# A hybrid trunk step on one core: the gated recurrence in pieces, the running sum of branches in DRAM, y split block by block

## The chip, the cores and the metric

One NeuronCore of a Trainium2 chip runs the whole kernel. The metric is the device time of one launch in microseconds. TensorE does matmuls, VectorE and GpSimd elementwise work, ScalarE activations; SyncE's queue (SP) issues every DMA.

## The reference, cut to what matters

Two layers over 1152 tokens (128 context tokens and 1024 latent ones), width 1024, everything in float32. In each layer one projection of the normed input h feeds three branches: A, windowed attention; B, a gated linear recurrence in both directions over 512 channels; C, differential attention. What a layer ends with is

```python
m = sigmoid(h @ w_merge)                   # three times 1024 columns
y = ( m[0] * ((oa * silu(g_a)) @ w_br_a)
    + m[1] * ((ob * silu(g_b)) @ w_br_b)
    + m[2] * ((oc * silu(g_c)) @ w_br_c))
x = x + gate * (y @ w_out)

# branch B, for each direction d
r, i = sigmoid(u @ wa + ba), sigmoid(u @ wx + bx)     # u: width-4 convolution of x_b
a = exp(-8 * r * softplus(-lam))
h_t = a_t * h_(t-1) + sqrt(1 - a_t**2) * (i * u)_t    # a scan along the tokens
```

The gate, and the shift and scale of the next layer's norm, come from a product of the conditioning vector with `mod_w`.

## The kernel before, in words

Every float32 operand of a matmul is split into a high and a low part (`split`, line 141: ScalarE copies the high part, GpSimd or VectorE subtracts), and `mm3` (L162) makes three matmuls of each product (L163, L164, L165). Tokens come in three chunks of 384, output columns in blocks of 128.

A layer has three stages. In `unit_phase` the attention branches are computed, and their gated outputs go to DRAM (`osp`), as do the inputs of the recurrence (`xsp`, `gsp`). In the **tail** there are 24 steps, eight column blocks j for each branch, in the order C, A, B. A step loads and splits its weights, and for each token chunk c runs a *merge* (24 matmuls against h, then a Tanh on ScalarE into `mg`, L971) and, one chunk behind (two from step 7 on), a *branch* (12 matmuls of the branch's output `oh`, `ol` with `wb`), whose result VectorE multiplies with `mg` and adds to the running sum `yr[j]` (L980 to L983, recorded at the helpers' lines L112 and L103). Eight `yr` tiles stay on chip until the end. Steps 22 and 23 (`tail_last`, L1018) do their six merges first, then for each chunk split all eight blocks of y. In **w_out** (L1060) y is multiplied with `w_out` in four column quarters, x is updated, and in the last quarter the next layer's h is made from it.

The recurrence (`lru`, L853) is done once for each of four column tiles `ct`: load x, weights, convolution into `u`, split of `u` (`luhl`), 48 matmuls into PSUM tag "t", Tanh, Exp, Tanh, Square, Sqrt, the scans (recorded at L860), the output to `osp[1]`. It is issued whole before steps 0, 2, 4 and 5 (`LRUN`), above the tail in priority, with its VectorE work at low priority (`late`, `LVO`).

`mod_chunk` (L295) makes three columns blocks of modulation: four or three loads of `mod_w`, 16 VectorE operations into `macc`, six small matmuls (L314). Layer 0 has eleven of them to do: four at steps 10, 13, 16 and 19 (`MODN`), seven in w_out (`MODW`).

A planner orders the instructions of each engine's queue: it plays the program through with its own idea of durations, and takes the ready instruction of the highest priority, which is its place in the program, moved forward by `tc.high_priority(offset)` (or back, with a negative one). Each engine then runs its queue strictly in that order. Tiles come from pools with a tag (`al`, sizes in `RINGS`, line 54): "S" has 26 tiles of 1152 columns, "P" 7, "W" 7 for weights, "D" 3, "Q" 2, "E" 2, "T" 2, "cx" and "tab" 1. An instruction whose tile finds none free is not placed until one is released. h holds 16 of the "S", a branch's output 8 tiles (`OTAG`, line 946).

Of the kernel before, what the change touches and what calls it, by code (L numbers as in the profile page):

```python
# [19 lines left out]
NTOK = 1152  # L20
# [10 lines left out]
LPO = 2500  # L31

LVO = -1600
# [31 lines left out]
def hybrid_dit_kernel(ctx, tc, I, O):  # L65
# [54 lines left out]
    xsp, gsp = (drp.tile([4, 128, NTOK], F32, name=n) for n in ("xsp", "gsp"))  # L120

# [731 lines left out]
    def lru(L, ct):  # L853
# [3 lines left out]

        def late(f, *args, **kw):
            with tc.high_priority(offset=LVO):
                f(*args, **kw)  # L860
        PIECES = ((0, 128), (128, 640), (640, NTOK))
        x = al("T", "lx", NTOK)

# [13 lines left out]
        A.activation(out=u, in_=x, func=AF.Identity, scale=cw(2), bias=cols[:, R_CB + ct:R_CB + ct + 1])  # L877
        for a0, a1 in PIECES:
            e0, e1 = (0, 128) if a0 == 0 else (128, NTOK)
            for j in (0, 1, 3):  # L880
                t0, t1 = max(a0, e0 + 2 - j), min(a1, e1 + 2 - j)
                late(stt, u[:, t0:t1], x[:, t0 + j - 2:t1 + j - 2], cw(j), u[:, t0:t1], ALU.mult, ALU.add)
        ra = [al("P", "lr", NTOK) for _ in range(2)]
        ri = [al("P", "li", NTOK), al("S", "li", NTOK)]
        for c in range(3):
            s = slice(384 * c, 384 * c + 384)
            uhl = al("D", "luhl", 2, 384)
            split(uhl[:, 0, :], uhl[:, 1, :], u[:, s])
            for d in range(2):
                for k, (dst, hb) in enumerate(((ra, D.hba), (ri, D.hbx))):  # L890
                    p = ps("t", 384)
                    m = 2 * k + d
                    mm3(p, wh[:, m, :], wl[:, m, :], uhl[:, 0, :], uhl[:, 1, :], True, True)
                    A.activation(out=dst[d][:, s], in_=p, func=AF.Tanh, scale=0.5,
                                 bias=hb[:, 4 * d + ct:4 * d + ct + 1])
                late(stt, ri[d][:, s], ri[d][:, s], 1.0, u[:, s], ALU.add, ALU.mult)
# [7 lines left out]
        for d in range(2):  # L904
            for c in range(2):
                s = slice(576 * c, 576 * c + 576)
                t = al("D", "lt2", 576)
                A.activation(out=t, in_=av[d][:, s], func=AF.Square)
                late(stt, ra[d][:, s], t, 1.0, ra[d][:, s], ALU.add, ALU.mult)
        for d in range(2):  # L910
            A.activation(out=ra[d], in_=ra[d], func=AF.Sqrt, scale=0.25)
        for d in range(2):
            a = av[d]
            st = cols[:, R_ST + 4 * d + ct:R_ST + 4 * d + ct + 1]
            for a0, a1 in PIECES if d == 0 else PIECES[:1] + PIECES[:0:-1]:
# [8 lines left out]
                if d:  # L924
                    s = slice(a1 - 1, a0 - 1 if a0 else None, -1)
                late(V.tensor_tensor_scan, out=ra[d][:, s], data0=a[:, s], data1=ri[d][:, s], initial=ini,
                     op0=ALU.mult, op1=ALU.add)
            e = 127 if d == 0 else 0
            late(V.tensor_copy, fin[:, 4 * d + ct:4 * d + ct + 1], ra[d][:, e:e + 1])
        res = ra[0]  # L930
        for c in range(3):
# [4 lines left out]
            late(stt, res[:, s], res[:, s], 0.5, g, ALU.mult, ALU.mult)  # L936
        dma(osp[1][ct], res)

# [7 lines left out]
    OTAG = {2: "SSSSSSSS", 0: "PPTTSSSS", 1: "SSSSSSSS"}  # L946

    def load_o(L, br):

        out = []  # L950
        for k in range(4):
            hi, lo = al(OTAG[br][2 * k], "oh", NTOK), al(OTAG[br][2 * k + 1], "ol", NTOK)
            out.append((hi, lo))
# [3 lines left out]
        return out  # L957
# [9 lines left out]
    YTAG = ["P", "P", "P", "P", "S", "Q", "Q", "tab"]  # L967
# [5 lines left out]
    def tail_branch(L, order, j, c, ohl, wb, m):  # L973
        p2 = ps("s", 384)
# [19 lines left out]
    def tail_step(L, br, order, j, o, lag):  # L994
# [3 lines left out]
        if order == 0:  # L998
            L.yr.append(al(YTAG[j], "yr", NTOK))
        for c in range(3):  # L1000
# [3 lines left out]
            def branch(c=c, m=m):  # L1004
                tail_branch(L, order, j, c, o[br], wb, m)
            L.late.append(branch)
            if len(L.late) > lag:
                L.late.pop(0)()

    def y_split(L, j, c):  # L1010
        if c == 0:
            th, tlo = {5: "SP", 6: "PP", 7: "QQ"}.get(j, "SS")
            L.y.append((al(th, "yh", NTOK), al(tlo, "yl", NTOK)))
# [4 lines left out]
    def tail_last(L, br, ohl):  # L1018

        ms = [al("T", "mg2", 3, 384) for _ in range(2)]  # L1020
        wbs = {}
        for j in (6, 7):
            mw = ws_load(w_in_cols(L.l, CMG + 1024 * br + 128 * j), KT)
            for c in range(3):
                tail_merge(L, br, j, c, mw, ms[j - 6][:, c, :])
# [246 lines left out]
```

## Time and profile before

| | us |
|---|---|
| median of 3 runs | 2887.47 (2887.15 to 2888.11) |
| the profiled execution | 2884.63 |
| its span | 2882.8 |
| TensorE busy in it | 2740.5 |
| VectorE busy | 1773.3 |
| ScalarE busy | 1284.2 |
| GpSimd busy | 924.8 |

The span goes from the first to the last instruction. PE is TensorE's matmuls, PEld its weight loads, DVE VectorE, ACT ScalarE, POOL GpSimd. Matmuls overlap in the pipeline, so a matmul's own duration is longer than the distance between two starts. The tail of layer 0 begins at about 807 us and its w_out at 1340, the tail of layer 1 at about 2240 and its w_out at 2770.

### The profile page before, as it was taken

How to read it: one execution, taken by the hardware profiler on the slowest of the kernel's cores; microseconds unless marked ns; L12 is line 12 of the kernel's file. 1: busy time of each engine (PE TensorE's matmuls, PEld its weight loads, DVE VectorE, ACT ScalarE, POOL GpSimd, SP SyncE). 2: the span in 40 equal slices, each digit the busy share in tenths (PEclk: the TensorE clock that was granted, in tenths of full speed). 3: DMA queues.
4: the chain of work that ended last, by engine and by line, in shares of the span. 5: the costliest groups of instructions: out<-in, count | busy, mean ns of one | idle time of the engine just before them, and what ended most of it. 6: DMA issues, size and time to landing. Idle time of an engine off the chain costs nothing.

```text
span 2882.8 us, 44242 instructions
## 1 busy us (share of the span) xinstructions
PE 2740.5 (95%) x16745; PEld 2648.5 (92%) x16745; DVE 1773.3 (62%) x4412; ACT 1284.2 (45%) x2577; POOL 924.8 (32%) x756
## 2 busy tenths in 40 slices
PE   8999999999998989998999999999999989999999
PEld 4889999999997989998989899998999989899989
DVE  5887878776646583116958887787665455311162
ACT  4464555566654631212144555555666456212110
POOL 1334354531234341213104252445212344322130
PEclk9999999999999999998999999999999999999999
DMA  6011011112222252114631010110112121311122
GB/s 228 25 33 34 19 32 42 36 48 74 70 73 65 65 159 68 52 39 144 195 100 36 22 34 19 33 48 31 55 64 80 63 70 60 114 44 49 49 90 85
DMA packets 231698, 190.74 MB, mean 66 GB/s; under 512 B 21746, under 2 KB 217660, under 8 KB 231484
## 3 DMA queue, kind: packets, MB, share of 16 engines
q1 hardware_dynamic: 231484, 187.92, 20.7%
q8 instruction: 131, 2.15, 0.3%
q14 instruction: 83, 0.68, 0.1%
HBM read 153.52 MB, written 34.35 MB: 65 GB/s over the span
## 4 chain that ended last, share of the span: by engine, by line
PE 71%; DVE 15%; ACT 5%; issue 4%; DMA 3%; POOL 1%; SPq 1%; DVEq 0%; ACTq 0%; POOLq 0%
PE ps_s L163 18%; PE ps_s L164 18%; PE ps_s L165 18%; PE ps_o L711 2%; PE ps_t L702 2%; DVE P L542 2%; PE ps_s L540 2%; DVE macc L112 2%; PE ps_t L569 1%; PE ps_s L541 1%; DMA modw<-in_mod_w_dram 1%; DVE lr L860 1%; DVE lr L112 1%; PE ps_o L164 1%; PE ps_s L662 1%
## 5 line engine op out<-in xcount | busy, mean ns | idle before, releaser
L163 PE MATMUL ps_s<-h,wsh 128*128 128x384 f32 x1920 | 660.0, 344 | 8.6 <-ACT mg L971 5.9
L165 PE MATMUL ps_s<-h,wsl 128*128 128x384 f32 x1920 | 654.4, 341 | 0.9 <-POOL wsl L103 0.9
L164 PE MATMUL ps_s<-h,wsh 128*128 128x384 f32 x1920 | 654.9, 341 | 0.0
L163 PEld LDWEIGHTS ps_s<-h,wsh 128*128 128x128 f32 x1920 | 364.3, 190 | 13.5 <-ACT mg L971 7.1
L165 PEld LDWEIGHTS ps_s<-h,wsl 128*128 128x128 f32 x1920 | 363.1, 189 | 2.0 <-POOL wsl L103 1.6
L164 PEld LDWEIGHTS ps_s<-h,wsh 128*128 128x128 f32 x1920 | 364.1, 190 | 0.6
L103 POOL TENSOR_TENSOR wsl<-wsraw,wsh 128x1024 fp32r<-128x1024 f32 x80 | 198.7, 2483 | 395.3 <-ACT wsh L100 229.6
L163 PE MATMUL ps_s<-uwh,h 128*128 128x384 f32 x864 | 296.9, 346 | 5.8 <-ACT h L100 2.8
L164 PE MATMUL ps_s<-uwl,h 128*128 128x384 f32 x864 | 293.9, 341 | 0.1
L165 PE MATMUL ps_s<-uwh,h 128*128 128x384 f32 x864 | 292.1, 344 | 0.0
L112 DVE SCALAR_TENSOR_TENSOR ps_s<-mg,ps_s 128x384 f32<-128x384 f32 x96 | 52.6, 559 | 359.7 <-PE ps_s L165 359.6
L103 POOL TENSOR_TENSOR qkraw<-qkraw,tab 128x384 f32<-128x384 f32 (+2 forms) x92 | 132.7, 1453 | 335.2 <-DVE qkraw L103 212.5
L542 DVE TENSOR_SCALAR_CACHE_REDUCE P<-ps_s 128x384 f32<-128x384 f32 (+1 forms) x400 | 205.5, 539 | 39.9 <-PE ps_s L541 38.7
L163 PE MATMUL ps_s<-oh,wb 128*128 128x384 f32 x576 | 196.0, 351 | 35.3 <-DVE yr L112 10.5
L103 DVE TENSOR_TENSOR PT<-ps_t,PT 128x512 fp32r<-128x512 f32 (+2 forms) x304 | 187.7, 625 | 59.5 <-ACT PT L100 58.0
L100 ACT ACTIVATE PT<-ps_t 128x512 fp32r<-128x512 f32 (+2 forms) x304 | 160.0, 546 | 125.1 <-PE ps_o L165 67.9
L552 ACT ACTIVATE P<-P,csm 128x1152 f32<-128x1152 f32 (+1 forms) x144 | 165.8, 1154 | 101.8 <-DVE csm L107 101.8
L164 PE MATMUL ps_s<-ol,wb 128*128 128x384 f32 x576 | 194.7, 346 | 0.0
L165 PE MATMUL ps_s<-oh,wb 128*128 128x384 f32 x576 | 194.5, 346 | 0.0
L971 ACT ACTIVATE mg<-ps_s 128x384 f32<-128x384 f32 x144 | 69.6, 485 | 266.1 <-PE ps_s L165 169.6
L163 PE MATMUL ps_s<-woh,yh 128*128 128x256 f32 x576 | 167.4, 291 | 11.7 <-DVE xt L103 6.5
L163 PEld LDWEIGHTS ps_s<-uwh,h 128*128 128x128 f32 x864 | 164.6, 191 | 9.4 <-ACT h L100 3.5
(253 smaller groups left out, 6364.6 us busy)
## 6 DMA issues: line engine op xcount, KB each, us to landing
wsraw<-in_w_in_dram SPq DMA_DIRECT2D x80, 512.0 KB, 3.7
wuraw<-in_w_in_dram SPq DMA_DIRECT2D x72, 192.0 KB, 3.5
ol<-osp SPq DMA_DIRECT2D x24, 576.0 KB, 5.0
modw<-in_mod_w_dram SPq DMA_DIRECT2D x16, 512.0 KB, 5.8
woraw<-in_w_out_dram SPq DMA_DIRECT2D x16, 512.0 KB, 4.4
modw<-in_mod_w_dram SPq DMA_DIRECT2D x14, 576.0 KB, 5.5
modw<-in_mod_w_dram SPq DMA_DIRECT2D x19, 384.0 KB, 4.3
wuraw<-in_w_in_dram SPq DMA_DIRECT2D x36, 128.0 KB, 2.3
```

The costliest lines, as they stand in the source:

```text
L100: A.activation(out=out, in_=in_, func=AF.Copy, scale=scale)
L103: e.tensor_tensor(out=out, in0=a, in1=b, op=op)
L112: V.scalar_tensor_tensor(out=out, in0=a, scalar=s, in1=b, op0=op0, op1=op1)
L163: T.matmul(out=out, lhsT=r(lh), rhs=r(rh), start=first, stop=False)
L164: T.matmul(out=out, lhsT=r(lh), rhs=r(rl), start=False, stop=False)
L165: T.matmul(out=out, lhsT=r(ll), rhs=r(rh), start=False, stop=last)
L540: T.matmul(out=p, lhsT=qh, rhs=kk, start=True, stop=False)
L542: V.tensor_scalar(out=S[:, n * c:n * c + n], in0=p, scalar1=1.0, scalar2=NEG, op0=ALU.mult, op1=ALU.max, accum_out=mx[:, mp, c:c + 1])
L552: A.activation(out=Ss[mp][:, 0:n], in_=Ss[mp][:, 0:n], func=AF.Exp, scale=0.125, bias=nm[:, mp:mp + 1], accum_out=acc)
L702: T.transpose(p[:, b, 128 * j:128 * j + 128], Ps[2 * t + j][:, (b0 + b) * 128:(b0 + b + 1) * 128], ident)
L711: T.matmul(out=po[:, t, :, :], lhsT=r(vs[kb]), rhs=r(x[:, b, :]), start=kb + k == 0, stop=k == 1 and kb == len(vs) - 1)
L971: A.activation(out=m, in_=p, func=AF.Tanh, scale=0.5)
```

## The change

- The recurrence becomes a generator (`recurrence`, with `lru` yielding at 11 places a tile). Four pieces are drawn at step 0, and one behind each chunk of a step, so that 41 chunks take the rest. All of it has the tail's priority; `late` is gone. The first two thirds of u are split in the pieces ahead of the matmuls. The final state is written out at its end.
- The running sum `yr[j]` has three buffers (two "Q", one "tab") instead of eight. After a block's last chunk in branch C and in branch A it is stored to `ysp` in DRAM; the next branch's step loads it again.
- In branch B a chunk of y is split as soon as it is complete, in `tail_branch`. Tiles of y come from "P" for blocks 0 and 1, from "S" for the others. `tail_last` takes the branches still due between its merges.
- Branch B's output is loaded in two parts, at steps 11 and 15; branch A's at step 7 as before. Tags change (`OTAG`).
- The branch's PSUM tile alternates between the tags "s" (four banks) and "o" (one).
- Modulation chunks: eight at steps 14 to 21, three in w_out. The weights of w_out use "S" tiles alone. The next layer's h takes y's tiles of blocks 2 to 5 for its first eight.

```diff
-LPO = 2500
-LVO = -1600
-MODN = (10, 13, 16, 19)
-LRUN = (0, 2, 4, 5)
-STO = 12
-MODW = ((0, 1), (0, 4), (0, 7), (1, 1), (1, 4), (1, 7), (2, 1), (2, 4))
+MODN = (14, 15, 16, 17, 18, 19, 20, 21)
+LRU0 = 4
+MODW = ((0, 2), (0, 6), (1, 1))
...
+    ysp = drp.tile([8, 128, NTOK], F32, name="ysp")
...
-    def alloc_h(L):
-        hs = [al("S", "h", 9, 128) for _ in range(2 * KT)]
+    def alloc_h(L, old=()):
+        hs = [t.rearrange("p (t n) -> p t n", n=128) for t in old]
+        hs += [al("S", "h", 9, 128) for _ in range(2 * KT - len(hs))]
...
         split(wh, wl, wr)
+        yield
...
+        def parts(c):
+            uhl[c] = al("D", "luhl", 2, 384)
+            split(uhl[c][:, 0, :], uhl[c][:, 1, :], u[:, 384 * c:384 * c + 384])
         for a0, a1 in PIECES:
...
-                late(stt, u[:, t0:t1], x[:, t0 + j - 2:t1 + j - 2], cw(j), u[:, t0:t1], ALU.mult, ALU.add)
+                stt(u[:, t0:t1], x[:, t0 + j - 2:t1 + j - 2], cw(j), u[:, t0:t1], ALU.mult, ALU.add)
+            if a0:
+                parts(0 if a0 == 128 else 1)
+                yield
-        ri = [al("P", "li", NTOK), al("S", "li", NTOK)]
+        ri = [al("P", "li", NTOK) for _ in range(2)]
         for c in range(3):
             s = slice(384 * c, 384 * c + 384)
-            uhl = al("D", "luhl", 2, 384)
-            split(uhl[:, 0, :], uhl[:, 1, :], u[:, s])
...
+            if c == 0:
+                parts(2)
+            yield
+            for d in range(2):
+                stt(ri[d][:, s], ri[d][:, s], 1.0, u[:, s], ALU.add, ALU.mult)
...
-        for d in range(2):
             for c in range(2):
...
+            yield
         for d in range(2):
             A.activation(out=ra[d], in_=ra[d], func=AF.Sqrt, scale=0.25)
+        yield
...
+            yield
         res = ra[0]
...
+    def recurrence(L):
+        for ct in range(4):
+            yield from lru(L, ct)
+        state_out(L)
+        yield
...
-    OTAG = {2: "SSSSSSSS", 0: "PPTTSSSS", 1: "SSSSSSSS"}
+    OTAG = {2: "SSSSSSSS", 0: "PPPSSSSS", 1: "SSSSSPPP"}
...
-    YTAG = ["P", "P", "P", "P", "S", "Q", "Q", "tab"]
+    YTAG = ("Q", "Q", "tab")
+    YSPL = ("PP", "PP", "SS", "SS", "SS", "SS", "SS", "SS")
...
-        p2 = ps("s", 384)
+        p2 = ps("so"[(j + c) % 2], 384)
...
             tt(V, yj, yj, p2, ALU.add)
+        if order < 2:
+            if c == 2:
+                dma(ysp[j], L.yr[j])
+        else:
+            y_split(L, j, c)
+
+    def y_tile(L, order, j):
+        L.yr[j] = al(YTAG[(8 * order + j) % 3], "yr", NTOK)
+        if order:
+            dma(L.yr[j], ysp[j])
...
             if len(L.late) > lag:
                 L.late.pop(0)()
+            next(L.rec, None)
...
-        ms = [al("T", "mg2", 3, 384) for _ in range(2)]
+        ms = [al("D", "mg2", 2, 384) for _ in range(3)]
...
+                if L.late:
+                    L.late.pop(0)()
         for j in (6, 7):
             wbs[j] = wbr_load(L, br, j)
+            y_tile(L, 2, j)
         for c in range(3):
-            for j in range(6):
-                y_split(L, j, c)
             for j in (6, 7):
-                tail_branch(L, 2, j, c, ohl, wbs[j], ms[j - 6][:, c, :])
-                y_split(L, j, c)
+                tail_branch(L, 2, j, c, L.o[br], wbs[j], m(j, c))
...
-        wtag = ("P", "S", "S", "P")
+        wtag = "SSSS"
...
-                alloc_h(Ln)
+                alloc_h(Ln, [t for j in range(2, 6) for t in L.y[j]])
...
+        L.rec = recurrence(L)
         for n, (br, order, j) in enumerate(steps):
...
+            with tc.high_priority(offset=TPO):
+                if n == 0:
+                    load_o(L, 2)
+                    for _ in range(LRU0):
+                        next(L.rec, None)
+                if n == 7:
+                    load_o(L, 0)
+                if n == 11:
+                    load_o(L, 1, (0, 1))
+                if n == 15:
+                    for _ in L.rec:
+                        pass
+                    load_o(L, 1, (2, 3))
...
```

## Rows read from the trace of the kernel before

**Rows 1.** The page: busy us of an engine, share of the span, instructions.

```profile
PE 2740.5 (95%) x16745; PEld 2648.5 (92%) x16745; DVE 1773.3 (62%) x4412; ACT 1284.2 (45%) x2577; POOL 924.8 (32%) x756
```

**Rows 2.** Stretches of the tails: length, busy us (instructions) of each engine, clock, DMA.

```profile
core 0: us, PE busy (x) PEld busy (x) DVE busy (x) ACT busy (x) POOL busy (x), PEclk, DMA share, GB/s
850.00:1050.00 200.00, 172.64 (x913) 168.47 (x913) 130.53 (x140) 112.07 (x145) 93.13 (x68) 0.94 0.29 91
1100.00:1300.00 200.00, 199.61 (x1138) 199.61 (x1139) 40.27 (x77) 35.78 (x57) 41.38 (x22) 1.00 0.17 49
2300.00:2500.00 200.00, 175.56 (x931) 172.05 (x930) 112.84 (x127) 102.94 (x138) 88.79 (x62) 0.93 0.27 84
```

**Rows 3.** TensorE's waits: us in total, times, longest us, over the whole span.

```profile
PE ps_t L163 <- ACT luhl L100: 20.1, 4, 5.8
...
PE ps_s L163 <- ACT mg L971: 12.5, 8, 3.1
PE ps_s L163 <- DVE yr L112: 10.5, 5, 3.8
...
PE ps_s L163 <- ACT oh L100: 8.4, 2, 4.7
...
PE ps_t L314 <- DVE macc L112: 1.8, 2, 1.1
```

**Rows 4.** TensorE in order of time in layer 0's recurrence: start, us, what.

```profile
876.81 1.33 PE L163 MATMUL ps_t<-luhl,gw 128*128 128x384 f32 x3 [5.77 <-ACT luhl L100]
...
878.25 0.52 PE L164 MATMUL ps_s<-h,wsh 128*128 128x384 f32 x1
878.57 0.52 PE L165 MATMUL ps_s<-h,wsl 128*128 128x384 f32 x1
```

**Rows 5.** Stretches of the tails' ends and of w_out; columns as above.

```profile
1326.00:1350.00 24.00, 17.07 (x84) 16.03 (x83) 24.00 (x27) 5.30 (x11) 16.40 (x8) 0.86 0.54 181
1350.00:1450.00 100.00, 92.38 (x724) 91.92 (x724) 91.71 (x188) 17.12 (x61) 17.47 (x6) 0.91 0.63 195
2751.00:2772.00 21.00, 15.30 (x77) 14.42 (x75) 21.00 (x24) 3.76 (x9) 15.42 (x8) 0.88 0.38 126
2822.00:2872.00 50.00, 50.00 (x423) 50.00 (x423) 14.45 (x34) 1.40 (x4) 0.00 (x0) 1.00 0.28 90
```

**Rows 6.** VectorE's costliest group, 1340 to 1450 us: busy us, mean ns, idle before.

```profile
L112 DVE SCALAR_TENSOR_TENSOR macc<-modw,sc,macc 128x384 f32<-128x384 f32 x98 | 70.9, 766 | 0.0
```

**Rows 7.** VectorE's groups in the tail without recurrence, 1100 to 1300 us.

```profile
L112 DVE SCALAR_TENSOR_TENSOR ps_s<-mg,ps_s 128x384 f32<-128x384 f32 x34 | 18.6, 561 | 155.6 <-PE ps_s L165 155.6
L103 DVE TENSOR_TENSOR yr<-yr,ps_s 128x384 f32<-128x384 f32 x34 | 18.3, 551 | 0.8
```

**Rows 8.** VectorE in order of time, scans of layer 1: start, us, what.

```profile
2446.13 3.25 DVE L860 TENSOR_TENSOR_SCAN lr<-la,lr,li 128x512 f32<-128x512 f32 x1
...
2454.07 1.49 DVE L860 TENSOR_TENSOR_SCAN lr<-la,li 128x128 f32<-128x128 f32 x1 [2.91 <-POOL li L103]
...
2455.67 2.06 DVE L860 TENSOR_TENSOR_SCAN lr<-la,cols,li 128x512 f32<-128x512 f32 x1
```

**Rows 9.** ScalarE in order of time, a table load in layer 1.

```profile
2439.32 1.28 ACT L911 ACT_TABLE_LOAD   x1
2440.61 1.17 ACT L911 ACTIVATE lr<-lr 128x1152 f32<-128x1152 f32 x1
```

**Rows 10.** ScalarE's groups of table loads, 840 to 1050 us: busy us, mean ns.

```profile
L911 ACT ACT_TABLE_LOAD x8 | 10.3, 1283 | 0.1
...
L971 ACT ACT_TABLE_LOAD x5 | 6.4, 1283 | 0.1
...
L902 ACT ACT_TABLE_LOAD x3 | 3.8, 1283 | 0.1
```

**Rows 11.** DMA issues: count, KB each, median us from issue to landing.

```profile
ol<-osp SPq DMA_DIRECT2D x24, 576.0 KB, 5.0
...
osp<-Oa SPq DMA_DIRECT2D x8, 576.0 KB, 3.4
```

More of the change, by code (lines that the diff above doesn't have):

```diff
@@ L892, in lru @@
                     m = 2 * k + d
-                    mm3(p, wh[:, m, :], wl[:, m, :], uhl[:, 0, :], uhl[:, 1, :], True, True)
+                    mm3(p, wh[:, m, :], wl[:, m, :], uhl[c][:, 0, :], uhl[c][:, 1, :], True, True)
                     A.activation(out=dst[d][:, s], in_=p, func=AF.Tanh, scale=0.5,
                                  bias=hb[:, 4 * d + ct:4 * d + ct + 1])
-                late(stt, ri[d][:, s], ri[d][:, s], 1.0, u[:, s], ALU.add, ALU.mult)
+            if c == 0:
[3 more added lines that the diff above has]
+                stt(ri[d][:, s], ri[d][:, s], 1.0, u[:, s], ALU.add, ALU.mult)
         av = []
@@ L907, in lru @@
                 t = al("D", "lt2", 576)
-                A.activation(out=t, in_=av[d][:, s], func=AF.Square)
-                late(stt, ra[d][:, s], t, 1.0, ra[d][:, s], ALU.add, ALU.mult)
+                A.activation(out=t, in_=a[:, s], func=AF.Square)
+                stt(ra[d][:, s], t, 1.0, ra[d][:, s], ALU.add, ALU.mult)
+            yield
         for d in range(2):
             A.activation(out=ra[d], in_=ra[d], func=AF.Sqrt, scale=0.25)
+        yield
         for d in range(2):
@@ L925, in lru @@
                     s = slice(a1 - 1, a0 - 1 if a0 else None, -1)
-                late(V.tensor_tensor_scan, out=ra[d][:, s], data0=a[:, s], data1=ri[d][:, s], initial=ini,
-                     op0=ALU.mult, op1=ALU.add)
+                V.tensor_tensor_scan(out=ra[d][:, s], data0=a[:, s], data1=ri[d][:, s], initial=ini,
+                                     op0=ALU.mult, op1=ALU.add)
             e = 127 if d == 0 else 0
-            late(V.tensor_copy, fin[:, 4 * d + ct:4 * d + ct + 1], ra[d][:, e:e + 1])
+            V.tensor_copy(fin[:, 4 * d + ct:4 * d + ct + 1], ra[d][:, e:e + 1])
+            yield
         res = ra[0]
@@ L944, in state_out, with load_o @@
         dma(O["nst"][0, L.l].rearrange("d (k n) -> (d k) n", n=128), so[0:8, :])
-    OTAG = {2: "SSSSSSSS", 0: "PPTTSSSS", 1: "SSSSSSSS"}
-    def load_o(L, br):
-        out = []
-        for k in range(4):
+    OTAG = {2: "SSSSSSSS", 0: "PPPSSSSS", 1: "SSSSSPPP"}
+    def load_o(L, br, ks=range(4)):
+        for k in ks:
             hi, lo = al(OTAG[br][2 * k], "oh", NTOK), al(OTAG[br][2 * k + 1], "ol", NTOK)
-            out.append((hi, lo))
+            L.o[br].append((hi, lo))
             dma(lo, osp[br][k])
@@ L956, in load_o @@
             tt(V if k % 2 else Pq, r(lo), lo, hi, ALU.subtract)
-        return out
     def wbr_cols(l, br, j):
@@ L992, in hybrid_dit_kernel, with tail_step @@
     MTAG = ("E", "E", "cx")
-    def tail_step(L, br, order, j, o, lag):
+    def tail_step(L, br, order, j, lag):
         mw = ws_load(w_in_cols(L.l, CMG + 1024 * br + 128 * j), KT)
         wb = wbr_load(L, br, j)
-        if order == 0:
-            L.yr.append(al(YTAG[j], "yr", NTOK))
+        y_tile(L, order, j)
         for c in range(3):
@@ L1004, in branch @@
             def branch(c=c, m=m):
-                tail_branch(L, order, j, c, o[br], wb, m)
+                tail_branch(L, order, j, c, L.o[br], wb, m)
             L.late.append(branch)
@@ L1132, in hybrid_dit_kernel @@
         L.l = l
-        L.yr, L.ssq, L.units, L.y, L.gates, L.late = [], [], [], [], [], []
+        L.yr, L.ssq, L.units, L.y, L.gates, L.late = [None] * 8, [], [], [], [], []
+        L.o = {br: [] for br in range(3)}
         Ls.append(L)
@@ L1218, in hybrid_dit_kernel @@
             with tc.high_priority(offset=TPO):
-                tail_step(L, br, order, j, o, 2 if n in LAG2 else MLAG)
-        while L.late:
-            L.late.pop(0)()
-        tail_last(L, 1, o[1])
+                tail_step(L, br, order, j, 2 if n in LAG2 else MLAG)
+        tail_last(L, 1)
         w_out_phase(L, Ls[l + 1] if l + 1 < DEPTH else None)
```

29 lines of the change are left out of this document (6 added, 23 removed).

## The prediction

> **What bounds the kernel now.** I read first the busy shares, then the stretches of equal length, then the waits of the engine that is left, and last the order of time in those places. TensorE is busy for 95% of the span [rows 1], so only the rest can be won, and the stretches say where it lies. Between the recurrence and the end of a tail, TensorE runs 1138 matmuls in 200 us, one each 0.1757 us, without a gap and at the full clock [rows 2]. In the 200 us in which the four recurrences are computed it runs 913 in layer 0 and 931 in layer 1, at a granted clock of 0.94 and 0.93 [rows 2]. No other engine is full there: VectorE has 131 of 200 us, ScalarE 112, GpSimd 93. So nothing is short of throughput; TensorE waits in its queue for things that come late. The waits name them: the split of the convolved input (luhl) 20.1 us in 4 waits, the sigmoid of the merge gate (mg) 12.5 us in 8, the running sum's write out of PSUM (yr, L112) 10.5 us in 5, the split of the next branch output (oh) 8.4 us in 2 [rows 3]. Each long wait costs more than itself: after 5.77 us without work the matmuls start 0.32 us apart instead of 0.18, the lower of the two clock levels (1.2 GHz against 2.4) [rows 4].
>
> Two more places are short. At the end of a tail VectorE is busy for all of the 24 us in layer 0 and all of the 21 us in layer 1 while TensorE gets 84 and 77 matmuls done [rows 5]; that is where all column blocks of y are split. And the first 100 us of w_out in layer 0 have 724 matmuls, where undisturbed w_out has 423 in 50 us [rows 5]; VectorE is 92 us busy there, 70.9 of them with the modulation chunks of the next layer [rows 6].
>
> **The change, part by part.**
>
> *Recurrence in pieces.* It removes no work. The missing matmuls are 1138 - 913 = 225 and 1138 - 931 = 207; times 0.1757 us that is 39.5 + 36.4 = 75.9 us, clock dips included. Now the same instructions come in 11 pieces for each of four column tiles, one behind each chunk of the tail, over 41 chunks (13.7 steps) of two branches. A chunk is 36 matmuls, 6.3 us. The load on VectorE of one recurrence is, from the difference of the stretches, (130.5 - 40.3)/4 = 23 us [rows 2], now beside 11 x 6.3 = 70 us, and the tail's own two operations take 0.56 + 0.55 us a chunk [rows 7]: VectorE fits twice. What made TensorE wait was order: the recurrence stood above the tail in priority, its VectorE work below it, so its matmuls entered the queue with no slack. Now the convolution and the split of the first two thirds are whole pieces ahead of the matmuls that read them, and I take the 20.1 us of luhl as gone. The same holds for mg and L112 as far as a long row of Exp, Tanh and Square no longer stands in front of the merge's Tanh.
>
> What stays: when branch A follows branch C, two of A's four tiles find no free buffer until C's last matmul (24 of 26 large buffers are held by h and C's output). The oh wait is of this kind: 8.4 us in two layers [rows 3], with a dip behind it; I keep 5 us a layer. The load itself is 5.0 us [rows 11], and one merge of 4.2 us covers most of it, so zero is possible, and 10 a layer is the other end (the stretch as it is now). For new waits of the pieces the trace has no row; the bounds are 0 and, from the longest tail wait on the scan's side (L112, 3.8 us), 8 scan pieces x 3.8 = 30 us a layer. I take 3 a layer, near zero, because an evacuation may be late by about two chunks: branch sums now alternate between two PSUM tags and five banks. Residue 2 x (5 + 3) = 16 us, gain 60 us.
>
> Here a rule stands against the pieces. Each Sqrt piece sits between Tanhs, so ScalarE changes tables twice: load, two Sqrts, load. In the trace a load is 1.28 us and the next operation starts 1.29 us after it [rows 9]; 16 of them (8 at L911, 5 at L971, 3 at L902) fall into layer 0's recurrence [rows 10]. One Sqrt piece is then 2 x 1.28 + 2 x 1.17 = 4.9 us, under the 6.3 us of a chunk, and two loads a tile make 8 instead of 16: no cost. The Trainium skill, "ScalarE: Activation LUTs", section on what ACT_TABLE_LOAD costs, puts a change of set at about 2.66 us, load and drain; by that the sum would be some 11 us smaller, an estimate. The trace shows no drain between the load and what follows, and I go by the trace; the other case is rival 5.
>
> *Running sum in DRAM.* Per layer 16 stores and 16 loads of 576 KB. Nearest rows: a store of that size lands after 3.4 us, a load after 5.0 [rows 11]; DMA's share in the steady tail is 0.17 [rows 2]. A step is 108 matmuls, 19 us; three buffers rotate, so a buffer has two steps, 38 us, for store and load. Cost 0 as long as the load is issued a few us early. If that cover is gone: the add waits, then the PSUM banks fill, two chunks (12 us) later TensorE stops. It adds waits on SP's queue, the only one that issues: a store waits for the last add of its block, and behind it stand the next weights. Bounds 0 and the rival below.
>
> *y split as each block is complete.* The end of the tail now has about half of the splits, since blocks 0 to 3 are split during steps that leave VectorE idle. Lost now: 24 - 14.1 = 9.9 us in layer 0 and 21 - 13.2 = 7.8 in layer 1 (84 and 77 matmuls at 0.176, a dozen and five of them at w_out's 50/423 = 0.118) [rows 5]. But block 4 finds no buffer until h is free after the last merge, and block 7's sum needs block 4's buffer before it can be loaded, 5 us. I keep 5 us in each layer: gain 4.9 + 2.8 = 7.7. Bounds: all 17.7 gained, or 6 us a layer lost if SP holds the load behind the w_out weights.
>
> *Modulation chunks.* Eight run in steps 14 to 21 and three in w_out, where seven did (98 operations, 14 each [rows 6]). In w_out 846 - 724 = 122 matmuls of 0.118 us are missing, 14.4 us [rows 5]; four sevenths is 8 us gained (bounds 0 and 14). In the tail, the eight find VectorE 80% idle; TensorE's in-order wait for their result is 1.8 us in 2 waits for eleven chunks now [rows 3]; I charge 2 us (bounds 0 and 8 x 1.1).
>
> *h in y's buffers, w_out weights in the large ring.* I cost these at nothing: layer 1's first GEMM already starts while w_out's last rows run.
>
> **Sum.** 75.9 - 16 + 7.7 + 8 - 2 = 73.6 us off the profiled execution's 2884.6 us (span 2882.8): 2811. The median of the runs shown is 2.9 us above that execution, so the forecast is 2887.5 - 73.6 = 2814.
>
> **Rivals.**
> 1. *The scans take the place of the old waits.* One scan piece is 1.49 + 2 x 2.06 = 5.6 us; beside a weight split on GpSimd a scan took 3.25 [rows 8], so 6.8, and with the chunk's 1.1 it is longer than the chunk's 6.3. VectorE takes its queue in order, so evacuations stand behind. For it: both tails wait at L112 now. Against: only 2 of 11 pieces are scans. At 2 us for each of 16 scan pieces: 32 us back, 2846.
> 2. *More is won.* Hand-over and new waits vanish and the tail's end is hidden: 16 + 10 us more, 2788.
> 3. *It doesn't spread.* The planner draws ready pieces forward, and TensorE's waits return; only the other gains stay, 7.7 + 8 - 2 = 13.7 us: 2874. Against: TensorE always has earlier work ready in the tail.
> 4. *Slower: the running sum's round trip sets the step.* Place: the add in steps 8 to 23, on SP's queue, where a store that waits for VectorE holds the loads behind it. 32 loads in two layers; beyond the cover of 12 us, each us late costs 32 us, so it decides from 73.6/32 = 2.3 us late beyond that cover. At 5 us late (one load's landing): 160 - 73.6 = 86 us slower, 2974. For it: one queue issues all. Against: DMA at 0.17, and 38 us of room.
> 5. *The table changes outlast the chunk.* Were a change to hold ScalarE for twice its 1.28 us, a Sqrt piece would take 4 x 1.28 + 2 x 1.17 = 7.5 us, 1.2 more than a chunk, and the merge's Tanh behind it would hold TensorE 8 times: 9 us, 2823. Against: the 1.29 us of [rows 9]. The Trainium skill's figure named above is of this kind.
>
> **How the numbers follow.** Forecast 0.55, rival 1 0.20, rival 2 0.07, rival 3 0.06, rival 4 0.07, rival 5 0.03, and 0.02 that all cancels. A change under 0.2% (5.8 us) can't be told from none. Faster 0.55 + 0.20 + 0.07 + 0.06 + 0.03 = 0.91, less 0.01 for rival 3's far edge = 0.90; same 0.03; slower 0.07. The range goes from rival 2 to past rival 1: 2784 to 2858, with rivals 3 and 4 and rival 1's far half left out, about 0.18.
>
> **What would show it.** Right: in the tails, steps of 19 us from the first on, with 1130 matmuls in any 200 us and a clock of 1.00; no luhl wait on TensorE; VectorE some 90 of 200 us over steps 0 to 13; w_out's first 100 us in layer 0 above 780 matmuls; TensorE idle only at the change from C to A and at the tail's end. Wrong: waits of TensorE on yr or on ps behind L860 in every fourth step (rival 1), on loads from ysp (rival 4), or the old stretch of 913 matmuls (rival 3).

## The result, and the profile after

The changed kernel takes 2911.9 us (three runs: 2911.2, 2911.9 and 2920.1), the kernel before 2887.8 beside it: a ratio of 1.009, 95% interval 1.0067 to 1.0113. A fourth run took 3355.3 us at a granted clock of 0.744 and is left out here; with it the median is 2916.0, and the expectations below reckon from that number. Forecast were 2814 us and a range of 2784 to 2858, so the change made the kernel slower by some 24 us instead of faster by 74. The profiled execution is the longest of the three, 2920.1 us, its span 2918.3.

Of the page: TensorE's busy time, its line of busy tenths, and the granted clock, both in 40 slices of 73 us.

```profile
PE 2746.5 (94%) x16745; PEld 2657.2 (91%) x16745; DVE 1767.2 (61%) x4412; ACT 1288.0 (44%) x2577; POOL 912.0 (31%) x756
...
PE   8999999999999999589999999999999999996999
...
PEclk9999999999999999799899999999999999997999
```

TensorE does the same work as in [rows 1], and there are two holes, one in each layer: the 17th slice (1167 to 1240 us) and the 37th (2626 to 2699). The stretches of [rows 2], same columns:

```profile
850.00:1050.00 200.00, 190.10 (x1052) 189.37 (x1051) 86.62 (x106) 101.62 (x140) 77.97 (x57) 0.97 0.32 107
1100.00:1300.00 200.00, 161.35 (x874) 158.39 (x874) 104.42 (x176) 50.27 (x74) 44.30 (x28) 0.88 0.39 121
2300.00:2500.00 200.00, 189.93 (x1053) 189.20 (x1053) 83.25 (x104) 97.75 (x135) 78.97 (x57) 0.97 0.32 104
```

Where the recurrence used to stand, TensorE now gets 1052 and 1053 matmuls done instead of 913 and 931. That is 261 more, and at 0.1757 us 46 us won. But the stretch that was undisturbed, 1138 matmuls, has 874: 264 missing, 46 us lost in layer 0 alone. TensorE's waits against [rows 3]:

```profile
PE ps_o L160 <- ACT oh L96: 25.2, 2, 16.4
PE ps_t L955 <- DVE fin L935: 25.1, 2, 12.6
PE ps_o L160 <- DVE yr L108: 13.2, 2, 6.7
PE ps_s L160 <- ACT mg L985: 12.5, 5, 5.4
PE ps_o L160 <- DVE yr L99: 10.3, 3, 5.1
PE ps_t L311 <- DVE macc L108: 7.9, 5, 4.7
...
PE ps_t L160 <- ACT luhl L96: 6.8, 2, 3.4
```

luhl fell from 20.1 to 6.8. In its place stand the final state (fin: the transpose behind the last scan) and the split of a branch's output (oh), 25 us each. TensorE in order of time shows that they are one place per layer, where branch B follows branch A (layer 0, then layer 1):

```profile
1196.32 0.37 PE L955 MATMUL ps_t<-ident,fin 128*8 128x128 f32 x1 [12.57 <-DVE fin L935]
1213.05 0.69 PE L160 MATMUL ps_o<-oh,wb 128*128 128x384 f32 x1 [16.36 <-ACT oh L96]
...
2654.51 0.37 PE L955 MATMUL ps_t<-ident,fin 128*8 128x128 f32 x1 [12.57 <-DVE fin L935]
2659.35 1.22 PE L1065 MATMUL ps_t<-ident,modt 128*128 128x128 f32 x4 [2.76 <-DVE so L957]
2669.39 0.69 PE L160 MATMUL ps_o<-oh,wb 128*128 128x384 f32 x1 [8.81 <-ACT oh L96]
```

Branch B's fourth tile is the last thing that the recurrence makes, and the recurrence is late. ScalarE's gate Tanhs of the fourth column tile (L895) show how late:

```profile
1111.44 0.58 ACT L895 ACTIVATE lr<-ps_t,hba 128x384 f32<-128x384 f32 x1
1156.36 0.58 ACT L895 ACTIVATE lr<-ps_t,hba 128x384 f32<-128x384 f32 x1
```

Three of the first chunk's four gate groups are done by 1112; the next Tanh of the recurrence runs 45 us later, and TensorE works on merges and branches in between. The last copy into fin says when the recurrence ends (VectorE's group, its first and last start):

```profile
L935 DVE COPY fin<-lr x8: 144/153/155, 882.4 to 1196.0; 128x1 f32<-128x1 f32 x8
```

1196 us, where it was 1021.9 in the kernel before. 41 chunks of 6.3 us, counted from the tail's first branch at 817, would have ended at 1075.

### The profile page after: what moved, and what is told of

Read it like the earlier page. It is cut to its first block, busy times and chain, and to the rows that moved or that the text cites. A ratio compares the mean times of both kernels' runs of the same rounds, so it can differ in the third digit from the quotient of the medians.

```text
span 2918.3 us, 44391 instructions
## 1 busy us (share of the span) xinstructions
PE 2746.5 (94%) x16745; PEld 2657.2 (91%) x16745; DVE 1767.2 (61%) x4412; ACT 1288.0 (44%) x2577; POOL 912.0 (31%) x756
## 5 line engine op out<-in xcount | busy, mean ns | idle before, releaser
L160 PE MATMUL ps_s<-h,wsh 128*128 128x384 f32 x1440 | 494.4, 344 | 12.4 <-ACT mg L985 10.5
L161 PE MATMUL ps_s<-h,wsh 128*128 128x384 f32 x1440 | 491.4, 341 | 0.0
L162 PE MATMUL ps_s<-h,wsl 128*128 128x384 f32 x1440 | 490.7, 342 | 0.5 <-POOL wsl L99 0.5
L160 PEld LDWEIGHTS ps_s<-h,wsh 128*128 128x128 f32 x1440 | 273.5, 190 | 15.4 <-ACT mg L985 11.7
L162 PEld LDWEIGHTS ps_s<-h,wsl 128*128 128x128 f32 x1440 | 273.1, 190 | 1.1 <-POOL wsl L99 0.8
L161 PEld LDWEIGHTS ps_s<-h,wsh 128*128 128x128 f32 x1440 | 273.2, 190 | 0.3
L160 PE MATMUL ps_s<-uwh,h 128*128 128x384 f32 x648 | 223.8, 347 | 2.5 <-ACT h L96 1.9
L162 PE MATMUL ps_s<-uwh,h 128*128 128x384 f32 x648 | 219.1, 346 | 0.0
L160 PE MATMUL ps_s<-yh,wsh 128*128 128x384 f32 x480 | 164.7, 344 | 3.0 <-ACT mg L985 2.0
L162 PE MATMUL ps_s<-woh,yl 128*128 128x256 f32 x576 | 164.5, 286 | 0.0
L161 PE MATMUL ps_s<-wol,yh 128*128 128x256 f32 x576 | 164.5, 286 | 0.0
L162 PE MATMUL ps_s<-yh,wsl 128*128 128x384 f32 x480 | 163.6, 341 | 0.5 <-POOL wsl L99 0.5
L161 PE MATMUL ps_s<-yl,wsh 128*128 128x384 f32 x480 | 163.0, 339 | 0.0
```

The source lines that it names most:

```text
L160: T.matmul(out=out, lhsT=r(lh), rhs=r(rh), start=first, stop=False)
L161: T.matmul(out=out, lhsT=r(lh), rhs=r(rl), start=False, stop=False)
L162: T.matmul(out=out, lhsT=r(ll), rhs=r(rh), start=False, stop=last)
```

## The experiments

All are timed against the kernel before, whose median beside them lay between 2887.6 and 2889.7; "changed kernel" is 2911.9, and since its three runs lie 9 us apart, a difference from it is good to a few us. The third column is the last copy into fin in layer 0, us.

| run | median us | fin |
|---|---|---|
| before | 2887.8 | 1021.9 |
| changed kernel | 2911.9 | 1196.0 |
| e1 four t banks, three s | 2900.5 | 1090.8 |
| e2 two pieces a chunk | 2929.1 | 1069.2 |
| e3 modulation chunks back | 2914.1 | 1195.8 |
| e5 fourth gate group in s | 2875.3 | 1104.3 |
| e8 state later | 2913.2 | 1194.3 |
| e9 pieces ranked higher | 2861.7 | 1047.2 |
| e10 branch sums in s alone | 2849.4 | 1127.5 |
| e11 e5 and e10 | 2892.7 | 1104.4 |
| e13 e9 and e10 | 2847.4 | 1054.4 |

**What is late, and what would have it early (e1, e2, e8).**

```diff
-    PSB = {"s": 4, "t": 3, "o": 1}
+    PSB = {"s": 3, "t": 4, "o": 1}
```

> Change against the changed kernel: four PSUM banks for tag t (gates, transposes) and three for tag s, instead of three and four. Theory A (banks): the four gate groups of a chunk rotate through three banks, the fourth waits for the first one's Tanh and is then put behind the merges and branches that the planner had already placed; so the recurrence slips by some 15 to 50 us a tile and ends 60 us late, at the change from branch A to branch B. With a bank for each of the four it ends around step 10 or 11 (some 1060 us), the stalls at 1183 and 1196 in layer 0 (12.9 and 16.7 us) and at 2642, 2656 and 2660 in layer 1 (12.9, 3.2 and 9.2 us) are gone, with the half clock behind them: 55 us and more, 2916 down to about 2860 (2845 to 2875). Rival B (buffers): the last tile waits for large buffers that branch A's output holds until step 15 ends; then the stalls stay, 2905 to 2925. Rival C: three s banks starve the merges and the time goes up, 2930.

Measured 2900.5: better by 11.4, not by 55. The stall at the change from A to B is gone, but the attention stages want four s banks:

```profile
PE ps_s L539 <- DVE P L541: 22.4, 24, 1.6
```

against 7.8 us in 14 waits in the changed kernel. The run shows that the pieces can be in time for branch B; it does not yet say what put them off.

```diff
             next(L.rec, None)
+            if br == 2:
+                next(L.rec, None)
```

> Change against the changed kernel: in the eight steps of branch C two pieces of the recurrence are drawn behind each chunk instead of one; nothing else. Theory A (banks) and rival D (the pieces are simply handed out too late) both want the recurrence done by step 9 or 10 and the stalls at the change from A to B gone, some 55 us; but TensorE then gets 24 gate groups in one bunch at the change from C to A and may wait there for the Tanhs, 10 to 20 us a layer: 2870 to 2890. Rival B (buffers): the last tile still ends with step 15 and the time stays at 2905 to 2925.

2929.1, worse than the changed kernel, though the recurrence ends at 1069. Drawn early, the gate groups of two tiles stand in one bunch at the change from C to A, and TensorE waits there for the split of the next tile, in both layers:

```profile
1039.88 1.33 PE L160 MATMUL ps_t<-luhl,gw 128*128 128x384 f32 x3 [29.67 <-ACT luhl L96]
```

An early end alone is not enough.

```diff
-        state_out(L)
-        yield
...
+                if n == 19:
+                    state_out(L)
```

> Change against the changed kernel: the transpose and store of the final state at step 19 instead of behind the last scan. TensorE waited 12.9 us in each layer for that transpose. If it is a wait of its own: 26 us less, 2890. If it only stands first in the queue in front of the wait for the split of branch B's last tile, which comes from the same late recurrence: that wait takes over, 2905 to 2918.

2913.2. The other wait takes over whole: layer 0's 12.6 and 16.4 us have become one of 29.1.

```profile
1181.78 0.34 PE L162 MATMUL ps_t<-luhl,gw 128*128 128x384 f32 x1
1211.20 0.69 PE L160 MATMUL ps_o<-oh,wb 128*128 128x384 f32 x1 [29.08 <-ACT oh L96]
```

**How much is the recurrence's (e4, e6).** Both leave the recurrence out, e4 (its edit is shown) of the changed kernel, e6 in the same way of the kernel before.

```diff
-            yield from lru(L, ct)
+            yield
+        V.memset(L.D.fin, 0.0)
...
-            dma(lo, osp[br][k])
+            dma(lo, gsp[k] if br == 1 else osp[br][k])
```

> Leaves out the whole recurrence (branch B reads the gate of the recurrence in its place); everything else of the changed kernel stays: running sum in DRAM, y split by blocks, modulation chunks, h in y's buffers. It shows what the rest of the change is worth. 288 gate matmuls go, 50.6 us. If the recurrence's stalls are the whole loss and the rest brings what I forecast: 2887.5 - 75.9 - 50.6 - 13.7 + 10 for the hand-over from C to A = 2757 (2745 to 2770). If the round trip of the running sum costs, it does so here too: every us late in the 32 loads adds 32 us, so 2790 or more, with TensorE waits on loads from ysp.

> The kernel before without its recurrence (branch B reads the gate of the recurrence in its place, the final state is zero). The changed kernel without it took 2769.5. The difference of the two is what the other parts of the change are worth. My working gave them 7.7 (y split) + 8 (modulation chunks in w_out) - 2 (in the tail) = 13.7 us, so 2783 (2775 to 2790). If those parts lose, below 2769. Against the kernel before it shows what the recurrence cost there: by the missing matmuls 75.9 us and 50.6 us of gate matmuls, 2761; the two figures do not fit together, and this run says which is off.

2769.5 for the changed kernel and 2763.8 (2757 to 2772) for the one before. The recurrence's 288 matmuls (36 a column tile, not the 48 said above) are 50.6 us; what it costs beyond them is 2889.7 - 2763.8 - 50.6 = 75.3 us before (2889.7 is the median beside that run) and 2911.9 - 2769.5 - 50.6 = 91.8 after. So the 75.9 us that I had read from missing matmuls were right, and instead of 60 of them being won, 16.5 more are lost. The rest of the change, for which I had 13.7 us, brings nothing: 2769.5 against 2763.8, and the runs of the two overlap.

**Is it the running sum, or the modulation chunks (e7, e3)?**

```diff
             dma(L.yr[j], ysp[j])
+            dma(L.yr[j], ysp[j])
```

> Change against the changed kernel: each column block of the running sum is loaded from DRAM twice, one load behind the other, into the same buffer (32 loads more in two layers, 18.9 MB). If the round trip lies beside other work, as I costed it: 2916, within 6 us. If the sum's transfers set the step (my rival 4), the second load's 5 us come on top in each of 32 steps: 3000 or more, with TensorE behind the add.

2923.2: 32 loads more cost some 9 to 11 us in all (by the means and by the medians), more than the 6 that I allowed and far from the 3000 us of rival 4, and no wait of TensorE names them. Rival 4 is out.

```diff
-MODN = (14, 15, 16, 17, 18, 19, 20, 21)
-MODW = ((0, 2), (0, 6), (1, 1))
+MODN = (10, 13, 16, 19)
+MODW = ((0, 1), (0, 4), (0, 7), (1, 1), (1, 4), (1, 7), (2, 1), (2, 4))
```

> Change against the changed kernel: the modulation chunks of the next layer back at their old places, four in the tail (steps 10, 13, 16, 19) and the rest in w_out, instead of eight in steps 14 to 21 and three in w_out. If the eight chunks cost what the trace after suggests (some 23 us of excess between 1225 and 1325 in layer 0, about half of it theirs) and w_out loses again what it had won (8 us by my working): between 2900 and 2912. If they cost nothing in the tail: 2916 + 8 = 2924. Layer 1 has no such chunks and must not move.

2914.1, no change that can be told: what the tail of layer 0 wins, w_out loses. In the profiled executions the first matmul of w_out comes 22 us earlier than in the changed kernel (1353.5 against 1376.0), layer 1's first merge Tanh only 8 us earlier (2262.5 against 2270.4).

**What puts the pieces off (e5, e9, e10, e11, e13).**

```diff
-                    p = ps("t", 384)
+                    p = ps("ttts"[2 * d + k], 384)
```

> Change against the changed kernel: the fourth gate group of each chunk (input gate of the backward direction) goes to a PSUM bank of tag s, the other three stay in t; the numbers of banks are untouched (s 4, t 3, o 1). With four t banks and three s (run before) the two tails took 42 us less and the two unit stages 25 us more. Theory A (the fourth gate group waits for a bank): the 42 us come again and the 25 do not, 2916 - 42 = 2874 (2862 to 2882); no wait on the state's transpose, no 13 and 17 us at the change from branch A to B. Rival B (buffers held by branch A's output): the stalls at that change stay, 2905 to 2925. Rival E (what helped was one s bank less, which slowed the merges): no gain.

2875.3, as theory A had it, and faster than before (0.9953, 0.9935 to 0.9971). Rival B falls: branch A's output holds the same buffers here.

```diff
-            next(L.rec, None)
+            with tc.high_priority(offset=1000):
+                next(L.rec, None)
```

> Change against the changed kernel: the pieces of the recurrence are ranked 1000 above the tail; banks as they are. Theory A holds that a gate group that has to wait for a bank is put off by tens of us because it has the same rank as the tail, whose later merges and branches then go first. With the higher rank it is taken as soon as its bank is free, the recurrence ends by step 10 and the stalls at the change from A to B go: 55 us and more won; but gate matmuls then stand early in TensorE's queue again, as in the kernel before, and wait for the split of the convolved input: 20 us lost. 2880 (2865 to 2895). If the number of banks alone sets it: 2905 to 2925.

2861.7 (0.9897, 0.988 to 0.9915), better than expected, with three t banks; TensorE's waits for luhl are 8.2 us, not the 20 that I feared. So the banks alone don't set it; a waiting gate group has to lose its turn as well.

```diff
-        p2 = ps("so"[(j + c) % 2], 384)
+        p2 = ps("s", 384)
```

> Undoes one part of the change: the branch sums go to tag s alone, as before, instead of to s and o in turn. Merges, and so the merge's Tanhs, then run less far ahead of the branches. If the putting off of the fourth gate group needs merges and branches that can be placed in its stead, there are fewer of them now: the recurrence ends around step 13, the stalls at the change from A to B go, 2875 (2865 to 2890). If the alternation hides late evacuations in the tail (two chunks of slack, as I worked with), every step loses some tenths of a us: 2890 to 2905. If it does neither: 2916.

2849.4 (0.9861, 0.9847 to 0.9876). One line of the change, the one that gives every second branch sum the bank of tag o, undone: 62.5 us less, below all three ranges, and the change is 38 us faster than before. The three stretches:

```profile
850.00:1050.00 200.00, 191.14 (x1054) 189.92 (x1053) 92.17 (x106) 100.74 (x137) 80.52 (x54) 0.97 0.33 109
1100.00:1300.00 200.00, 188.40 (x1070) 184.66 (x1069) 130.64 (x224) 53.77 (x81) 56.27 (x33) 0.98 0.47 147
2300.00:2500.00 200.00, 188.94 (x1053) 187.41 (x1052) 94.94 (x116) 88.02 (x120) 80.68 (x57) 0.98 0.35 113
```

The first and third are those of the changed kernel, what was won there stays; the second has 196 matmuls more.

> The fourth gate group in tag s (2875.3 by itself) and the branch sums in tag s alone. If the alternation of the branch sums brings something of its own: 2880 to 2895. If not, and its only effect is on the order of the gates: 2865 to 2878.

2892.7, inside the range for an alternation that brings something of its own. But e10 shows that it brings nothing, and here the two edits together are slower than either alone, which neither case explains. As in e5, the recurrence begins before the attention stage is over, and here TensorE waits 10.4 us in layer 0 and 10.5 in layer 1 (at 2263) for its first split, 3.8 each in e5. Against e10 its waits for VectorE's sums (yr, L108) are 22.4 us instead of 12.9, those for the merge's Tanh 19.1 instead of 9.1. So two repairs together make a worse order; why the planner makes it is not shown.

> Branch sums in tag s alone (2849.4 by itself) and the pieces ranked 1000 above the tail (2861.7 by itself). If both do the same thing, letting the recurrence end before branch B begins, they do not add: 2845 to 2862. If each takes away another part of the loss: about 20 us more, 2830.

2847.4 (0.9854, 0.9834 to 0.9874): e9 and e10 take away the same loss and don't add. The four column tiles of layer 0 show where each of them works (the second of a tile's two copies into fin, us):

| run | first | second | third | fourth |
|---|---|---|---|---|
| changed kernel | 892 | 986 | 1056 | 1196 |
| e5 fourth gate group in s | 862 | 943 | 1014 | 1104 |
| e9 pieces ranked higher | 886 | 933 | 986 | 1047 |
| e10 branch sums in s alone | 886 | 986 | 1053 | 1127 |

The rank brings the second, third and fourth tile forward. Without the alternation the second and third tile are as late as in the changed kernel; only the fourth comes 69 us earlier. That is early enough for branch B, and in e13 an end at 1054 instead of 1127 wins nothing more.

**Is the alternation bad by itself (e14, e15)?** e14 puts the alternating line into the kernel before; e15 undoes it in the changed kernel without a recurrence.

> One part of the change alone: the kernel before with its branch sums in tags s and o in turn. Theory F (the alternation is bad by itself: it lets the planner place merges in pairs and branches in pairs, so that the in-order queue has work in it that waits): slower by 10 us or more, 2900 and up. Theory A (it is bad only where pieces of the tail's own rank are to come between): no change, within 6 us of 2888; the recurrence there stands above the tail. If it helps as I thought (evacuations may be late by two chunks): 2875 to 2882.

> Leaves out the recurrence as in the run of the changed kernel without it (2769.5), and undoes the alternation of the branch sums. Theory A: without a recurrence the alternation has nothing to put off; within 6 us of 2769.5, and the 66.6 us that undoing it won are all the recurrence's. Theory F: it costs by itself, 2745 to 2760. If it hides evacuations: 2778 or more.

e14: 2903.2, 15.6 us slower (1.0055, 1.0037 to 1.0074), as theory F had it. e15: 2763.7, 5.8 faster than e4, just inside theory A's 6 us. So the alternation costs something by itself, up to 15.6 us, and the other 47 to 57 us of the 62.5 only together with the pieces. The steady tail of e14 shows how it costs, TensorE and then ScalarE in order of time:

```profile
1193.13 0.34 PE L164 MATMUL ps_o<-ol,wb 128*128 128x384 f32 x1
1193.31 0.34 PE L165 MATMUL ps_s<-oh,wb 128*128 128x384 f32 x1
1193.48 0.34 PE L165 MATMUL ps_o<-oh,wb 128*128 128x384 f32 x1
1194.82 0.44 PE L163 MATMUL ps_s<-h,wsh 128*128 128x384 f32 x1 [1.00 <-ACT mg L971]
...
1194.28 0.96 ACT L971 ACTIVATE mg<-ps_s 128x384 f32<-128x384 f32 x2 [6.13 <-DVE ps_s L112]
```

Two branch sums with banks of their own run matmul by matmul in turn and end together. Only then does VectorE read the `mg` tiles that they need, so the merge's Tanh waits 6.1 us for a free one, and TensorE waits for that Tanh: five times, 4.2 us together, in the 200 us from 1100, where the kernel before has one wait of 1.2 us. The stretches of e14, and behind them the last one in the kernel before:

```profile
850.00:1050.00 200.00, 177.84 (x948) 175.39 (x946) 131.16 (x142) 118.07 (x153) 98.27 (x69) 0.94 0.28 87
1100.00:1300.00 200.00, 194.96 (x1102) 193.03 (x1102) 39.74 (x75) 34.61 (x55) 39.43 (x21) 1.00 0.17 51
2300.00:2500.00 200.00, 179.46 (x963) 177.37 (x963) 122.34 (x137) 118.72 (x155) 96.78 (x70) 0.94 0.28 90
2540.00:2740.00 200.00, 192.74 (x1081) 189.90 (x1080) 33.72 (x61) 34.76 (x54) 39.15 (x21) 1.00 0.15 43
...
2540.00:2740.00 200.00, 200.00 (x1135) 200.00 (x1134) 34.53 (x63) 36.51 (x60) 40.79 (x22) 1.00 0.17 49
```

The steady tails lose 36 and 54 matmuls, 15.8 us, but beside the recurrence, which stands above the tail here, e14 has 35 and 32 more than [rows 2], 11.8 us. So the run's 15.6 us are not the steady tails alone; where the rest of them lies was not worked out.

**The modulation chunks again (e12, e16, e17).** e12 is e5 with the tail's chunks ranked 800 lower (MPO = -800); e16 is e10 with the places of e3; e17 is e13 with the tail's modulation weights loaded into tag T, three row blocks at a time:

```diff
-        m = 3 if tag == "S" else 2
+        wt = "T" if tag == "D" else tag
+        m = 3
...
-            w = al(tag, "modw", k1 - k0, 128 * n)
+            w = al(wt, "modw", k1 - k0, 128 * n)
```

> The fourth gate group in tag s (2875.3 by itself) and the modulation chunks of the tail ranked 800 lower. In that kernel TensorE loses 4.8 + 2.3 + 1.5 us in layer 0 before the chunks' own matmuls and 5.3 + 1.7 + 5.6 us behind VectorE between 1130 and 1245. If the chunks cause these by standing in VectorE's and TensorE's queues too early: 12 to 20 us less, 2855 to 2863. If the same work only comes to stand elsewhere: 2870 to 2880. Layer 1 must not move.

> Branch sums in tag s alone (2849.4 by itself), and the modulation chunks back at their old places. By my working the new places bring 8 us in w_out and cost 2 in the tail: 2855. In the run with the recurrence late, moving them back changed nothing (2914 against 2916). If they are a wash here too: 2849, within 5 us.

> Branch sums in tag s alone and the pieces ranked higher (2847.4 so far), and the modulation chunks of the tail load their weights into the two buffers of tag T, which the recurrence has left by then, three row blocks to a load instead of two, so that a load can be under way before the chunk ahead is done. In the changed kernel VectorE sits idle 23.4 us between 1200 and 1376 us in front of a chunk's operation whose weights have not landed, with branch evacuations behind it in its queue. If that costs TensorE: 6 to 12 us less, 2836 to 2841, and less idle time of VectorE there. If TensorE's other work covers it: 2847, within 4 us. Layer 1 must not move.

e12: 2870.2, 5 us less than e5, inside the range for work that only comes to stand elsewhere. e16: 2867.9, 18.5 us slower than e10: with the recurrence in time the new places are worth 18.5 us, not 6. The profiled execution of e16 reaches w_out 4 us later than that of e10 (1340.0 against 1336.3) and layer 1's first merge Tanh 19 us later (2245.8 against 2226.7), so most of it lies behind w_out's start. e17: 2844.1 (0.9852, 0.9829 to 0.9875). VectorE's idle time in front of the chunks' operations but the first, 1060 to 1341 us, fell from 34.7 us (e13) to 1.9 us (e17; in front of the first it rose from 2.2 to 10.4),

```profile
L108 DVE SCALAR_TENSOR_TENSOR macc<-modw,sc,macc 128x384 f32<-128x384 f32 (+1 forms) x112 | 70.8, 688 | 1.9 <-DMA modw<-in_mod_w_dram 1.7
```

and the time by 3.3 us, which the spread of the two runs doesn't tell from none: little of that wait reached TensorE. e17 has the lowest median of all versions.

## Why the prediction was wrong

**The recurrence in pieces.** What it cost before was right (75.9 forecast, 75.3 measured). Most of the reading of its old place was right too: luhl's 20.1 us fell to 6.8, and 46 us came back there. But the stretches reach 1052 and 1053 matmuls at a clock of 0.97, not the 1130 at 1.00 that I named as a sign; the waits on mg (12.5 us before and after) and on the running sum (L112, now L108: 10.5 and 13.2) did not fall as I had hoped. What failed are two steps. "I take 3 a layer, near zero, because an evacuation may be late by about two chunks: branch sums now alternate between two PSUM tags and five banks" counted the alternation as help; it is the edit that costs 62.5 us. My upper bound for new waits, 30 us a layer, comes close to what the change from A to B costs, 12.6 + 16.4 in layer 0 and 12.6 + 2.8 + 8.8 in layer 1, with lower clock behind them, but by luck: it was made of evacuations behind scans, and these are waits for the end of the recurrence. And "over 41 chunks (13.7 steps)" took the chunk at which a piece is issued for the time at which it runs. The pieces have the tail's own rank; between two gate Tanhs of the fourth tile TensorE does 45 us of merges and branches, and the last piece ends 121 us after its place (1196 against 1075). Without the alternation the pieces cost 2849.4 - 2763.7 - 50.6 = 35.1 us, so 40 are won where I had 60: of the forecast's own size, two thirds.

Not settled is why the planner places gate groups so late, and later still when the branch sums alternate. Shown is that a rank above the tail brings all tiles after the first forward, that a bank in s for the fourth gate group ends the recurrence 92 us earlier, and that undoing the alternation brings the fourth tile alone forward; which resource a gate group waited for in the planner's account was not.

**The change from C to A.** I kept 5 us a layer for buffers; TensorE waits 6.5 us there in layer 0 and 6.7 in layer 1, for another reason, so that the size came out by luck. VectorE in order of time in the changed kernel:

```profile
995.50 7.99 DVE L108 SCALAR_TENSOR_TENSOR lu<-lx,cols,lu 128x126 f32<-128x126 f32 x7
1003.41 0.54 DVE L108 SCALAR_TENSOR_TENSOR yr<-mg,ps_o 128x384 f32<-128x384 f32 x1
```

Seven convolution operations stand in front of an evacuation. In e10, where TensorE waits 5.9 us, it is the scans, after 7.2 us of waiting for GpSimd in the queue:

```profile
984.68 1.48 DVE L932 TENSOR_TENSOR_SCAN lr<-la,li 128x128 f32<-128x128 f32 x1 [7.22 <-POOL li L99]
986.19 0.15 DVE L935 COPY fin<-lr 128x1 f32<-128x1 f32 x1
986.26 2.03 DVE L932 TENSOR_TENSOR_SCAN lr<-la,cols,li 128x512 f32<-128x512 f32 x1
988.39 2.05 DVE L932 TENSOR_TENSOR_SCAN lr<-la,lr,li 128x512 f32<-128x512 f32 x1
990.37 0.52 DVE L108 SCALAR_TENSOR_TENSOR yr<-mg,ps_s 128x384 f32<-128x384 f32 x1
```

That is rival 1, in one place a layer and not in 16.

**Running sum in DRAM.** Costed at 0. Stores land after 3.1 us, loads after 3.8, and no wait of TensorE names them; if the first 32 loads cost what the second 32 did in e7, the round trip still takes about 10 us, an estimate that no run took apart:

```profile
ysp<-yr SPq DMA_DIRECT2D x32, 576.0 KB, 3.1
yr<-ysp SPq DMA_DIRECT2D x32, 576.0 KB, 3.8
```

**y split.** The tails' ends are as forecast or better. The 24 and 21 us around the start of w_out (at 1376.0 and 2800.1), and w_out, against [rows 5]:

```profile
1358.00:1382.00 24.00, 22.70 (x145) 22.50 (x143) 17.22 (x19) 5.01 (x11) 9.30 (x5) 1.00 0.39 120
1386.00:1486.00 100.00, 95.32 (x739) 95.14 (x740) 63.55 (x122) 20.25 (x68) 17.84 (x7) 0.92 0.50 153
2783.00:2804.00 21.00, 21.00 (x134) 21.00 (x134) 14.96 (x19) 3.91 (x8) 7.20 (x5) 1.00 0.34 109
```

145 and 134 matmuls for 84 and 77. But some of it is given back a few us on, behind the first window (moved by 4 us it holds 123 matmuls), where a branch sum waits for VectorE after w_out has begun; in e10 that wait is 0.3 us:

```profile
1385.82 0.69 PE L160 MATMUL ps_o<-oh,wb 128*128 128x384 f32 x1 [5.11 <-DVE yr L99]
```

**Modulation chunks.** Eight were to cost 2 us in the tail and w_out to win 8. By e16 they win 18.5 together once the recurrence is in time, and nothing while it is late (e3). In the changed kernel itself the 100 us of w_out have 739 matmuls for 724, not the 780 that I named as a sign. In the changed kernel VectorE idles 23.4 us between 1200 and 1376 in front of a chunk's operation whose weights are still on their way, evacuations behind it:

```profile
L108 DVE SCALAR_TENSOR_TENSOR macc<-modw,sc,macc 128x384 f32<-128x384 f32 (+1 forms) x112 | 74.3, 718 | 23.4 <-DMA modw<-in_mod_w_dram 23.4
```

I had charged TensorE's wait for the chunk's result, and not VectorE's for its weights.

**The sum.** Recurrence +40, alternation -62.5, the rest 0 (e15 takes 2763.7, the kernel before without its recurrence 2763.8): -22, measured -24.1. Forecast were +60 and +13.7. The three terms are differences of the same runs, so that they add up is no test of them; the 2 us left over are the scatter of the kernel before. If the modulation chunks are worth their 18.5 us without a recurrence too, other parts of the rest lose about as much; no run took them apart.

**Rivals 3 and 5.** The pieces were spread, so not rival 3; they were put off, which no rival said, and none of the signs that I named for being wrong was the hole at the change from A to B. Of table loads there are 15 in the first layer's recurrence (840 to 1200 us), not the 8 that I counted, each still 1.28 us:

```profile
L916 ACT ACT_TABLE_LOAD x8 | 10.3, 1283 | 0.1
L985 ACT ACT_TABLE_LOAD x3 | 3.8, 1283 | 2.1 <-DVE fin L935 2.1
L895 ACT ACT_TABLE_LOAD x3 | 3.8, 1283 | 0.1
...
L907 ACT ACT_TABLE_LOAD x1 | 1.3, 1283 | 0.0
```

The merge's Tanh (mg) holds TensorE 12.5 us as before, so rival 5 is not seen. The 2.66 us that the Trainium skill ("ScalarE: Activation LUTs", section "What ACT_TABLE_LOAD costs") gives for a load and a drain do not show here: after 11 of the 15 loads the next operation starts 1.29 or 1.30 us after the load began, and at the other four it waits for another engine.

## What to carry to other kernels

Work that is cut into pieces and given the rank of the work around it need not run where it is issued (here the last piece came 121 us later): before counting on a spread, find the step by which its last result is needed, and give the pieces a rank above their surroundings (e9) so that one that misses its turn gets the next. A second bank for alternate results is not slack by itself: it also lets two results run in turn and end together (e14), and changes which work is ready. And a wait that stands first in a queue is worth nothing until the one behind it is known (e8: 12.6 and 16.4 us became 29.1).

## What was not expected of the hardware

The running sum's DMA has room left: 32 more loads of 576 KB cost about 0.3 us each (e7), and the median load went from 3.8 to 4.6 us. After TensorE's two waits at 1183 to 1213 us the granted clock of the 200 us around them is 0.88, and it is 0.98 in e10, where they are missing.
